# Transposes of an expert's activations placed between the products of a pair's sums

## The chip, the cores and the metric

The kernel runs on one core of one Trainium2 chip. The metric is the device time of one execution in microseconds (us); the median of several runs is compared. One more execution was taken with the hardware profiler on, and all rows below come from it.

## The reference

One layer of a streaming-encoder block over 512 tokens of width 1024: pooling and differential attention, cross-attention over 256 memory tokens, then a mixture of 32 experts of which each token takes four. The change lies in the experts alone:

```python
def expert_block(args):
    tok, g, e = args
    xb = xt[tok]
    hb = clamped_swiglu(xb @ w_gu[e] + b_gu[e])
    yb = hb @ w_down[e] + b_down[e]
    return yb * g[:, None].astype(yb.dtype)

y = jnp.zeros((T, D), h.dtype).at[row_tok].add(y_rows.reshape(n_rows, D).astype(h.dtype))
```

Here `T` is 512 and `D` is 1024; the tokens of an expert are gathered, go through gate-up, the clamped SwiGLU and down, are scaled by their gate and added back into `x`.

## The kernel before

The dense layers run first (`dense`, to about 410 us), then `experts` walks over the 32 experts, one stage for each, and a last stage without a gate-up. An expert has room for 96 tokens: a first part of 64 and a second part of 32, and the second part's products stand in a conditional block (`when`), entered only if the expert has more than 64 tokens. Weights come as 1 MB tiles in 17 shared buffers, eight `gu` tiles and four `dnw` tiles an expert, loaded by SyncE's queue as buffers come free.

Stage `e` runs gate-up of expert `e` and then down of expert `e - 1`. On TensorE its order is, as the code is written: the small products of `dispatch(e + 2)` that find slots and gates (tile `slots`), eight transposes of the gathered tokens (`to_features`: `xgT` in PSUM, then two VectorE multiplies at line 1010 write `xT`), six transposes of the activations of expert `e - 1` (`turn_act`: four into one PSUM tile `actT`, two into another, each copied to SBUF tile `aT` by one ScalarE instruction at line 1102), eight small products that put the biases into PSUM (`biases`), gate-up of the first part (`gate_up1`, weight tiles j = 0 to 7), gate-up of the second part (`gate_up2`), and `down`, which reads `aT`.

Experts go in pairs: `sums` gives each pair its tiles `ya`, `yb` and the one-hot `ohc`, which `down` fills through `split` (a ScalarE copy at line 120, then a VectorE subtraction at line 121, on the same PSUM bank). In an odd stage with `e > 2`, after j = 3, `combine_half` adds the pair before into `x`: for each of four token tiles `i` and two halves `h`, three products (`sum_up`'s parts) go into a PSUM tile `comb1`, and VectorE adds that to `x` (line 1162). There are 15 such stages (e = 3, 5, ..., 31) with 24 products and 8 additions each.

TensorE's order is the order in which the code is written: `queued` puts every matmul and transpose behind the one before. The other engines' instructions are put in order by the framework's scheduler, which works with times of its own; a few are pinned to their written place (`keep_in_program_order`, the scaling of the gathered tokens at line 999 among them).

PSUM tiles made by `bank` share four buffers (`ps1`), those made by `pair` share two. During gate-up one of the four holds the second part's accumulator (`pc`), so `comb1` turns over the other three; `actT`, `slots` and the two tiles of `down` come from the same four.

Of the kernel before, what the change touches and what calls it, by code (L numbers as in the profile page):

```python
# [24 lines left out]
KT = D // P  # L25
# [35 lines left out]
class Block:  # L61
# [904 lines left out]
    def slots(self, pt, n):  # L966

        nc = self.nc
        t = self.ms.tile([P, n, 2, 6], F32, name="slots")
        nc.vector.tensor_copy(t, pt)  # L970
        tok = self.ms.tile([P, n, 2], F32, name="tok", bufs=5)
        nc.vector.scalar_tensor_tensor(tok, t[:, :, :, 1], float(P), t[:, :, :, 0], op0=OP.mult, op1=OP.add)
        gat = self.ms.tile([P, n, 2], F32, name="gat", bufs=5)
        nc.vector.tensor_tensor(gat, t[:, :, :, 2], t[:, :, :, 3], op=OP.add)
        nc.vector.tensor_tensor(gat, gat, t[:, :, :, 4], op=OP.add)
        gi = self.ms.tile([CAP, n], I32, name="gi", bufs=5)
        nc.vector.tensor_copy(gi[0:64], tok[0:64, :, 0])
        nc.vector.tensor_copy(gi[64:96], tok[64:96, :, 1])

        nc.vector.scalar_tensor_tensor(tok, tok, -1.0, t[:, :, :, 5], op0=OP.add, op1=OP.add)  # L980
        return gi, gat, tok
# [114 lines left out]
    def turn_act(self, act, n):  # L1096
        nc = self.nc
        pt = self.bank("actT", (P, 4, P))
        for c in range(n):
            self.tr(pt[:, c], act[:, c * P:(c + 1) * P], self.ident)  # L1100
        aT = self.mw.tile([P, n, P], F32, name=f"aT{n}", bufs=1)
        nc.scalar.activation(aT, pt[:, :n], AF.Copy)  # L1102
        return aT

    def sums(self):

# [45 lines left out]
        nc = self.nc  # L1152
        self.add_sums(i, self.sum_up(i, self.pair("comb"), parts, True, True))

    def combine_half(self, i, h, parts):

        ps, n = self.bank("comb1"), len(parts)
        for k, (y, oh) in enumerate(parts):
            self.mm(ps, oh[:, i * P:(i + 1) * P], y[h] if isinstance(y, list) else y[:, h], start=k == 0,
                    stop=k == n - 1, skip_group_check=True)  # L1160
        xi = self.x_sb[:, i, 512 * h:512 * h + 512]
        self.nc.vector.tensor_tensor(xi, ps, xi, op=OP.add)  # L1162

# [12 lines left out]
    def experts(self):  # L1176
        nc = self.nc
        disp, xTs, xgs = {}, {}, {}

        def gather(e):  # L1180
            xgs[e] = self.gather(disp[e][0])

        def slots(e):
            return [t[:, 0] for t in disp[e][1:]]

        xTs[0] = self.first_features()
        acts, parts, xg = {}, {}, None
        for e in range(NE + 1):


            if e == 0:
                biases = self.load_down_biases()
            if e == 1:
                biases = self.down_biases(biases)
                for i in range(NT):
                    self.combine(i, [biases])
            if 0 < e < NE - 2:
                disp[e + 2] = self.dispatch(e + 2, 1)
            if 0 < e < NE:
                xTs[e] = self.to_features(xg)  # L1200
            if e:
                aT = [self.turn_act(t, n) for t, n in zip(acts.pop(e - 1), (4, 2))]

            if e < NE:
                gu = self.gu.pop(e)
                cond = lambda e=e: self.when(self.flag(e))
                if e + 1 < NE:
                    self.load_gate_up(e + 1)
                    if e:
                        gather(e + 1)  # L1210
                self.load_down(e)
                xT = xTs.pop(e)
                pa, pc = self.biases(self.pick[:, e:e + 1])
                for j in range(KT):
                    self.gate_up1(pa, xT, gu[j], j)
                    if e == 0 and j == 0:
                        self.count()
                    if e == 0 and j == 1:
                        disp[1] = self.dispatch(1, 1)
                        gather(1)  # L1220
                    if j == 3 and e % 2 and e > 2:
                        for i in range(NT):
                            for h in range(2):
                                self.combine_half(i, h, parts[e // 2 - 1])
                    if e == 0 and j in (1, 3, 5):
                        with cond():
                            for k in range(j - 1, j + 1):
                                self.gate_up2(pc, xT, gu[k], k)
                    if e == 0 and j == 2:
                        disp[2] = self.dispatch(2, 1)  # L1230
                    if j == 5 and e == 0:
                        disp[0] = self.dispatch(0, 1)
                        biases = self.round_down_biases(biases)
                    if j == 6 and e + 1 < NE:
                        xg = self.normed(xgs.pop(e + 1))
                act = self.swiglu(pa[:, 0], pa[:, 1], 512)
                with cond():
                    for k in range(0 if e else 6, KT):
                        self.gate_up2(pc, xT, gu[k], k)
                acts[e] = act, self.swiglu(pc[:, 0], pc[:, 1], 256)  # L1240

            if e:
                f = e - 1
                r = slice(64 * (f % 2), 64 * (f % 2) + 64)
                if f % 2 == 0:
                    parts[f // 2] = self.sums()
                p = parts[f // 2]
                self.down(*aT, self.dnw.pop(f), *slots(f), lambda f=f: self.when(self.flag(f)),
                          p[2 * (f % 2)], [t[r] for t in p[1]], last=e == NE)
        self.finish(parts[NE // 2 - 1])  # L1250
        self.overflow()
# [33 lines left out]
    def overflow(self):  # L1285
# [15 lines left out]
        n = nc.values_load(self.more[0:1, 0:1], min_val=0, max_val=NT * P * 4 // CAP)  # L1301
        with self.tc.For_i(0, n, 1):
# [14 lines left out]
            t = self.slot("own_t", [P, NT, NE])  # L1317
# [5 lines left out]
            with nc.allow_low_precision(reason="sums of one term that is not zero"):  # L1323
                for i in range(NT):
                    t = self.slot("own_v", [P, 6, NE])
# [4 lines left out]
            t = self.slot("own_p", [96, NE])  # L1330
# [4 lines left out]
            e = ms.tile([P, 1], F32, name="own_e", bufs=1)  # L1335
# [8 lines left out]
            w = []  # L1344
# [6 lines left out]
            gi, gat, tok = self.slots(pt, 1)  # L1351
# [4 lines left out]
                self.gate_up2(pc, xT, w[j], j)  # L1356
            act = self.swiglu(pa[:, 0], pa[:, 1], 512)
            act2 = self.swiglu(pc[:, 0], pc[:, 1], 256)
            aT, aT2 = self.turn_act(act, 4), self.turn_act(act2, 2)
            a, c, _ = self.sums()  # L1360
            c = [v[0:64] for v in c]
            self.down(aT, aT2, w[KT:], gat[:, 0], tok[:, 0], nullcontext, a, c)
            self.finish([a, c])

    def run(self):
# [41 lines left out]
```

## Time and profile before

| | us |
|---|---|
| median of 3 runs | 1485.63 |
| lowest, highest | 1483.84, 1486.21 |
| the profiled execution | 1483.18 |
| its span, first to last instruction | 1480.9 |

In that span TensorE (PE) is busy for 1428.7 us, VectorE (DVE) 700.9, ScalarE (ACT) 392.5, GpSimd (POOL) 31.8. The DMA engines move 455.61 MB, 307 GB/s of them from and to HBM over the span.

How to read the rows further down: PE is TensorE's matmuls, PEld its weight loads, which run beside the matmuls. Times in a timeline are in us from the start of the span, and successive instructions of one kind stand in one row, marked with x and their count. A matmul's duration holds its way through the array, so neighbours overlap; the distance from one start to the next is what the stream costs. Square brackets give the idle time of the engine ahead of the instruction and what ended it. Out<-in names the tile written and the tiles read; tile `gu` covers the weight tiles and both PSUM accumulators of gate-up, `comb` stands for `comb1`.

### The profile page before, as it was taken

How to read it: one execution, taken by the hardware profiler on the slowest of the kernel's cores; microseconds unless marked ns; L12 is line 12 of the kernel's file. 1: busy time of each engine (PE TensorE's matmuls, PEld its weight loads, DVE VectorE, ACT ScalarE, POOL GpSimd, SP SyncE). 2: the span in 40 equal slices, each digit the busy share in tenths (PEclk: the TensorE clock that was granted, in tenths of full speed). 3: DMA queues.
4: the chain of work that ended last, by engine and by line, in shares of the span. 5: the costliest groups of instructions: out<-in, count | busy, mean ns of one | idle time of the engine just before them, and what ended most of it. 6: DMA issues, size and time to landing. Idle time of an engine off the chain costs nothing. (4 is left out here: it accounts for less than half of the span.)

```text
span 1480.9 us, 22050 instructions
## 1 busy us (share of the span) xinstructions
PE 1428.7 (96%) x8940; PEld 744.3 (50%) x8940; DVE 700.9 (47%) x1700; ACT 392.5 (27%) x692; POOL 31.8 (2%) x49
## 2 busy tenths in 40 slices
PE   8999999999979999999999999999999999999994
PEld 7878788888333434344343443434343434434342
DVE  6857956452443534244353443433453434444334
ACT  6346635342112211111222121121212121121213
POOL 0000000000000000000000000000000000000000
PEclk9999999999989999999999999999999999999997
DMA  7222315066839898999999999999999999999941
GB/s 228 93 89 86 115 61 164 29 256 242 330 128 394 358 396 349 386 355 409 397 405 406 400 408 407 408 371 398 409 380 406 392 396 399 405 397 401 408 189 58
DMA packets 84310, 455.61 MB, mean 308 GB/s; under 512 B 14201, under 2 KB 14722, under 8 KB 35042
## 3 DMA queue, kind: packets, MB, share of 16 engines
q1 hardware_dynamic: 79330, 439.16, 75.0%
q0 software_dynamic: 3472, 12.29, 2.7%
q10 hardware_dynamic: 1392, 2.51, 0.5%
q8 instruction: 86, 1.41, 0.4%
q14 instruction: 30, 0.25, 0.0%
HBM read 449.71 MB, written 4.21 MB: 307 GB/s over the span
## 5 line engine op out<-in xcount | busy, mean ns | idle before, releaser
L107 PE MATMUL gu<-gu,xT 128*64 128x512 f32 (+1 forms) x3200 | 577.1, 594 | 3.2 <-DVE xT L1010 2.2
L107 PEld LDWEIGHTS gu<-gu,xT 128*64 128x64 f32 (+1 forms) x3200 | 177.5, 127 | 377.2 <-issue 349.8
L107 PE MATMUL down<-dnw,aT 128*32 128x256 f32 (+1 forms) x2288 | 300.0, 476 | 7.6 <-PEq L102 6.8
L1058 DVE TENSOR_SCALAR g<-gu 128x256 f32<-128x256 f32 x64 | 32.7, 552 | 392.7 <-PE gu L107 285.7
L107 PEld LDWEIGHTS down<-dnw,aT 128*32 128x32 f32 (+1 forms) x2288 | 120.7, 122 | 183.6 <-issue 145.4
L1060 ACT ACTIVATE s<-g 128x256 f32<-128x256 f32 x64 | 33.5, 523 | 386.0 <-DVE g L1058 385.9
L1162 DVE TENSOR_TENSOR x<-comb,x 128x512 f32<-128x512 f32 x120 | 82.0, 689 | 94.7 <-PE comb L107 94.6
L999 ACT ACTIVATE xg<-xg 96x1024 f32<-96x1024 f32 x31 | 35.7, 1150 | 246.3 <-DMA xg<-x_rows,gi 246.3
L120 ACT ACTIVATE yb<-down,gat 32x256 fp32r<-32x256 f32 x128 | 59.5, 465 | 124.6 <-DVE yb L121 86.0
L121 DVE SCALAR_TENSOR_TENSOR yb<-down,gat,yb 32x256 fp32r<-32x256 f32 x128 | 61.6, 482 | 55.0 <-ACT yb L120 53.5
L107 PE MATMUL comb<-ya,yb 128*128 128x512 f32 x256 | 83.5, 397 | 0.0
L118 DVE TENSOR_TENSOR w_lo<-w,w_hi 128x1024 fp32r<-128x1024 f32 x56 | 67.0, 1218 | 10.4 <-ACT w_hi L117 10.0
L120 ACT ACTIVATE ya<-down,gat 64x512 fp32r<-64x512 f32 x64 | 43.7, 683 | 65.6 <-PE down L107 64.8
L107 PEld LDWEIGHTS comb<-ya,yb 128*128 128x128 f32 x256 | 48.0, 188 | 22.7 <-issue 13.0
L117 ACT ACTIVATE w_hi<-w 128x1024 fp32r<-128x1024 f32 x56 | 56.7, 1052 | 4.2 <-DMA w<-in_w_ckv_dram 1.6
L121 DVE SCALAR_TENSOR_TENSOR ya<-down,gat,ya 64x512 fp32r<-64x512 f32 x64 | 48.0, 751 | 14.1 <-ACT ya L120 12.0
L107 PE MATMUL comb<-yb,ohc 128*128 128x512 f32 x128 | 49.9, 390 | 0.0
L1064 DVE TENSOR_TENSOR g<-gu,s 128x256 f32<-128x256 f32 x64 | 49.2, 844 | 1.5 <-ACT s L1060 1.5
L992 POOL DMA_INDIRECT xg<-x_rows,gi x31 | 28.5, 918 | 969.9 <-PE actT L111 508.0
L1102 ACT ACTIVATE aT<-actT 128x512 f32<-128x512 f32 x64 | 31.1, 489 | 43.7 <-PE actT L111 42.9
L111 PE MATMUL xgT<-ident,xg 96*128 96x96 f32 x256 | 36.0, 284 | 0.8 <-DVE xg L1031 0.8
L1010 DVE TENSOR_TENSOR xT<-xgT,g_ffn 128x384 f32<-128x384 f32 x64 | 34.7, 553 | 1.7 <-PE xgT L111 0.8
(340 smaller groups left out, 1676.8 us busy)
## 6 DMA issues: line engine op xcount, KB each, us to landing
gu<-in_w_gu_dram SPq DMA_DIRECT2D x256, 1024.0 KB, 17.4
dnw<-in_w_down_dram SPq DMA_DIRECT2D x128, 1024.0 KB, 19.9
w<-in_w_ckv_dram SPq DMA_DIRECT2D x8, 1024.0 KB, 5.2
w<-in_w_in_dram SPq DMA_DIRECT2D x7, 1024.0 KB, 5.8
w<-in_w_out_dram SPq DMA_DIRECT2D x4, 1024.0 KB
w<-in_w_cq_dram SPq DMA_DIRECT2D x4, 1024.0 KB, 6.2
w<-in_w_co_dram SPq DMA_DIRECT2D x4, 1024.0 KB
x<-in_x_dram SPq DMA_DIRECT2D x8, 256.0 KB, 6.0
```

What stands on the lines that cost most here:

```text
L107: self.pin(self.nc.tensor.matmul(*a, **k))
L111: self.pin(self.nc.tensor.transpose(*a))
L117: self.pin(nc.scalar.activation(hi, src, AF.Copy))
L118: self.pin(nc.vector.tensor_tensor(lo, src, hi.bitcast(F32), op=OP.subtract))
L120: nc.scalar.activation(hi, src, AF.Copy, scale=scale)
L121: nc.vector.scalar_tensor_tensor(lo, src, scale, hi.bitcast(F32), op0=OP.mult, op1=OP.subtract)
L999: self.nc.scalar.activation(xg[:, :D], xg[:, :D], AF.Copy, scale=xg[:, D:D + 1]))
L1010: nc.vector.tensor_tensor(xT[:, c], pt[:, c, :CAP], self.g3[:, c, None].to_broadcast([P, 4, CAP]), op=OP.mult)
L1058: nc.vector.tensor_scalar(g, gate, LIMIT, None, op0=OP.min)
L1060: nc.scalar.activation(s, g, AF.Sigmoid, scale=ALPHA)
L1064: nc.vector.tensor_tensor(g.rearrange("s (j b p) -> s j p b", p=P, b=2), r(up), r(s), op=OP.mult)
L1162: self.nc.vector.tensor_tensor(xi, ps, xi, op=OP.add)
```

## The change

`turn_act` becomes a generator that yields after each transpose, and `turn_acts` runs it for both activations and leaves the copied tiles in `self.aT`. In even stages, in stage 1 and in `overflow` it is run to its end at once, where the transposes stood before. In odd stages with `e > 2` nothing is transposed ahead of gate-up; `combine_half` instead takes one step of the generator after each of its products, from the second half of the first token tile on. With three products a half, the six transposes follow the three products of (i 0, h 1) and the three of (i 1, h 0); the copy of the first four comes with the fifth step, that of the last two with the seventh, after the first product of (i 1, h 1).

```diff
         for c in range(n):
             self.tr(pt[:, c], act[:, c * P:(c + 1) * P], self.ident)
+            yield
         aT = self.mw.tile([P, n, P], F32, name=f"aT{n}", bufs=1)
         nc.scalar.activation(aT, pt[:, :n], AF.Copy)
-        return aT
+        self.aT.append(aT)
+
+    def turn_acts(self, acts):
+
+        self.aT = []
+        for act, n in zip(acts, (4, 2)):
+            yield from self.turn_act(act, n)
...
-    def combine_half(self, i, h, parts):
+    def combine_half(self, i, h, parts, between):
...
                     stop=k == n - 1, skip_group_check=True)
+            if i or h:
+                next(between, None)
...
+            turned = None
             if e:
-                aT = [self.turn_act(t, n) for t, n in zip(acts.pop(e - 1), (4, 2))]
+                turned = self.turn_acts(acts.pop(e - 1))
+                if e == 1 or e % 2 == 0:
+                    for _ in turned:
+                        pass
...
-                                self.combine_half(i, h, parts[e // 2 - 1])
+                                self.combine_half(i, h, parts[e // 2 - 1], turned)
...
-                self.down(*aT, self.dnw.pop(f), *slots(f), lambda f=f: self.when(self.flag(f)),
+                self.down(*self.aT, self.dnw.pop(f), *slots(f), lambda f=f: self.when(self.flag(f)),
```

The rest of the diff gives `overflow`, which no token enters unless an expert has more than 96, the same generator run to its end.

## Rows read from the trace of the kernel before

**Rows 1.** The page: busy time (share of span, instructions); costliest groups.
```profile
PE 1428.7 (96%) x8940; PEld 744.3 (50%) x8940; DVE 700.9 (47%) x1700; ACT 392.5 (27%) x692; POOL 31.8 (2%) x49
...
L107 PEld LDWEIGHTS comb<-ya,yb 128*128 128x128 f32 x256 | 48.0, 188 | 22.7 <-issue 13.0
```

**Rows 2.** Waits, 425 to 1445 us: who waited for what, total us, times, longest.
```profile
PEld gu L107 <- DVE xT L1010: 15.5, 26, 0.7
...
PEld gu L107 <- DMA gu<-in_w_gu_dram: 3.9, 13, 0.4
...
PE gu L107 <- DVE xT L1010: 2.2, 12, 0.2
```

**Rows 3.** Timeline of PE, start of stage 5: start, us, instruction, idle before it.
```profile
546.65 1.10 PE L111 MATMUL xgT<-ident,xg 96*128 96x96 f32 x8
547.59 0.82 PE L111 MATMUL actT<-ident,g 128*128 128x128 f32 x6
548.34 0.95 PE L107 MATMUL gu<-bias,pick 96*32 96x512 bf16 x8
549.48 7.09 PE L107 MATMUL gu<-gu,xT 128*64 128x512 f32 x32 [0.19 <-DVE xT L1010]
```

**Rows 4.** Timeline of DVE, the same stretch.
```profile
547.37 0.28 DVE L961 TENSOR_SCALAR oh<-iota,slot_no 128x256 bf16<-128x256 bf16 x1
547.69 0.74 DVE L121 SCALAR_TENSOR_TENSOR ya<-down,gat,ya 64x512 fp32r<-64x512 f32 x1
548.46 0.16 DVE L975 TENSOR_TENSOR gat<-gat,slots 128x2 f32<-128x2 f32 x1
...
548.87 0.56 DVE L1010 TENSOR_TENSOR xT<-xgT,g_ffn 128x384 f32<-128x384 f32 x1
...
549.99 0.76 DVE L121 SCALAR_TENSOR_TENSOR ya<-down,gat,ya 64x512 fp32r<-64x512 f32 x1
```

**Rows 5.** Timeline of ACT, stage 5 to the end of its sums.
```profile
546.54 0.68 ACT L120 ACTIVATE ya<-down,gat 64x512 fp32r<-64x512 f32 x1 [0.31 <-PE down L107]
548.29 0.60 ACT L1102 ACTIVATE aT<-actT 128x512 f32<-128x512 f32 x1 [1.07 <-PE actT L111]
548.91 0.68 ACT L120 ACTIVATE ya<-down,gat 64x512 fp32r<-64x512 f32 x1
...
558.52 1.15 ACT L999 ACTIVATE xg<-xg 96x1024 f32<-96x1024 f32 x1 [8.52 <-DMA xg<-x_rows,gi]
```

**Rows 6.** Timeline of PE, the sums of stage 5 (first, last and what follows).
```profile
556.50 0.50 PE L107 MATMUL comb<-ya,yb 128*128 128x512 f32 x1
556.84 0.39 PE L107 MATMUL comb<-yb,ohc 128*128 128x512 f32 x1
...
557.53 0.40 PE L107 MATMUL comb<-yb,ohc 128*128 128x512 f32 x1
...
562.17 1.08 PE L107 MATMUL gu<-gu,xT 128*64 128x512 f32 x4
```

**Rows 7.** Timeline of DVE, the additions of stage 5.
```profile
557.50 4.78 DVE L1162 TENSOR_TENSOR x<-comb,x 128x512 f32<-128x512 f32 x7 [6.24 <-PE comb L107]
```

**Rows 8.** Timeline of PE in the dense part: transposes amid products of the sums' kind.
```profile
356.95 0.39 PE L107 MATMUL cops<-w_hi,col 128*128 128x512 f32 x1
357.18 0.60 PE L111 MATMUL h3T<-ident,x 128*128 128x128 f32 x4
357.53 0.47 PE L107 MATMUL cops<-w_hi,coh 128*128 128x512 f32 x1
357.85 0.39 PE L107 MATMUL cops<-w_lo,coh 128*128 128x512 f32 x1
```

**Rows 9.** Timeline of PE, start of gate-up in stage 31.
```profile
1405.02 0.95 PE L107 MATMUL gu<-bias,pick 96*32 96x512 bf16 x8
1405.80 7.04 PE L107 MATMUL gu<-gu,xT 128*64 128x512 f32 x32
```

**Rows 10.** Timeline of DVE, start of stage 31.
```profile
1404.91 1.02 DVE L1010 TENSOR_TENSOR xT<-xgT,g_ffn 128x384 f32<-128x384 f32 x2
```

More of the change, by code (lines that the diff above doesn't have):

```diff
@@ L1358, in overflow @@
             act2 = self.swiglu(pc[:, 0], pc[:, 1], 256)
-            aT, aT2 = self.turn_act(act, 4), self.turn_act(act2, 2)
+            for _ in self.turn_acts((act, act2)):
+                pass
             a, c, _ = self.sums()
             c = [v[0:64] for v in c]
-            self.down(aT, aT2, w[KT:], gat[:, 0], tok[:, 0], nullcontext, a, c)
+            self.down(*self.aT, w[KT:], gat[:, 0], tok[:, 0], nullcontext, a, c)
             self.finish([a, c])
```

## The prediction

> **What bounds the kernel now.** I read the page first: TensorE is busy for 1428.7 us of a span of 1480.9 [rows 1], so a change pays only where it shortens TensorE's own stream or a wait of it. The waits over the experts come next: of all the stretch the one that repeats is gate-up waiting for `xT`, 26 times on the weight load, at most 0.7 us, and part of it shows on the matmuls too; waits for weights are at most 0.4 us each [rows 2]. So in the experts TensorE sets the pace, DMA keeps ahead of it, and each stage has one small hole, at the start of gate-up. I then read the timelines of the three engines side by side around that hole and around the sums of stage 5, which stands for the odd stages.
>
> At the start of stage 5 the six transposes take TensorE from 547.59 to 548.34, 0.75 us. The bias products follow, and gate-up starts at 549.48, marked as waiting for `xT` [rows 3]. VectorE's first `xT` multiply runs from 548.87 for 0.56 us, to 549.43, and gate-up follows 0.05 us later: this multiply, not the transposes, lets gate-up start. What holds the multiply is VectorE's own queue: ahead of it stand the one-hots of a dispatch, the subtraction for `ya` (from 547.69 for 0.74 us) and small instructions for gates and indices from 548.46 on [rows 4]. Its input, the `xgT` transposes, is done before 547.8 (the eight start at 546.65 and last 1.10 us) [rows 3]. Nothing on that path reads `actT`.
>
> **What the change removes.** Six transposes, 0.75 us, leave the start of 15 odd stages. The bias products then start about 0.65 to 0.75 us earlier, but gate-up still waits for the `xT` multiply, whose predecessors on VectorE are fed by the down products' end (ScalarE's first `ya` copy at 546.54 [rows 5]), not by what was removed. So the hole grows by what was taken out, and in 14 stages I count a gain of 0.00 us. In stage 31, which has no dispatch left, `xT` is free earlier: the first multiply starts at 1404.91 [rows 10], and with 0.56 us for it and 0.05 to follow gate-up could start at 1405.52 against 1405.80 [rows 9]: a gain of 0.28 us, once.
>
> ScalarE loses the copy of `aT` at 548.29 that stands ahead of its second `ya` copy at 548.91 [rows 5]. That second copy shares a PSUM bank with VectorE's `ya` subtraction, which ends at 548.43 [rows 4], so it can move forward by some 0.45 us at most; who needs it is only the second `ya` subtraction, which is due after `xT`. Worth nothing by itself, and a risk (second rival).
>
> **What it adds.** The same six transposes now stand between products of the sums. First, their price on TensorE. The products run 0.23 us from start to start (three of them from 556.84 to 557.53 [rows 6]; the whole 24 from 556.50 to 562.17, 5.67 us). The trace has no lone transpose between two such products, but it has four in a row between products of the same shape and type in the dense part: from the product at 356.95 to the second product after them at 357.85 pass 0.90 us [rows 8], of which two product distances of 0.227 are not theirs, so 0.446 us for four, 0.11 each. The change of kind is in that: 0.23 from product to transpose, and after the transposes the first product is followed by the next only after 0.32 instead of 0.23 us. A lone transpose pays the change each time, so I bound it from 0.11 (the run's mean) to 0.14 (a run's mean plus one more 0.03 us change) and take 0.12: 6 x 0.12 = 0.71 us a stage.
>
> Can VectorE's additions hide that? Seven of them take 4.78 us, 0.683 each [rows 7], and three products take 0.68. The products are not held by the additions by more than 8 x 0.683 - 24 x 0.227 = 0.02 us a stage, so there is no slack to hide 0.71 us in. Nothing below zero is likely here either: a transpose can't make a product shorter.
>
> On weight loads a page speaks against the change. The rows show that the four transposes and the change of kind cost 0.446 us, no more than transposes do among themselves (0.75 us for six, 0.125 each, at the start of stage 5 [rows 3]). The Trainium skill, page "TensorE: Matmul & The Clock Gate", section "Measured speedup vs the span model", states that a weight load overlaps running matmuls only where its row group differs; ours all use 128 rows. By that rule a product's weight load (188 ns [rows 1]) would stick out behind each transpose of about 0.11 us by 0.08 us, 0.47 us a stage more; the rows on the four transposes speak against it, since they leave room for 0.03 at most. It is the third rival.
>
> Second, PSUM. Three of the four banks turn over in this stretch, and `actT` now takes two of the turns that were `comb1`'s. I lay the stage out from its start at 0, with the distances above, additions of 0.69 us that start 0.04 after the last product of a half ends, and a ScalarE copy of 0.60 us [rows 5]. Products of (0,0) start at 0, 0.34, 0.57; its addition runs 1.00 to 1.69 (as in rows 7: 557.50 is 1.00 after 556.50). Half (0,1) and its three transposes run 0.80 to 1.76; half (1,0) takes the first bank at 1.76, just free. The fourth transpose at 2.07 lets ScalarE copy from about 2.45 to 3.05. The fifth, due at 2.42, needs a bank: the one of (0,1) whose addition starts at 1.92 and ends at 2.61, so it waits about 0.25 us. Half (1,1), due at 3.06, takes the bank of the first `aT` copy at about 3.12: 0.07 more. After that banks are free in time. Together 0.32 us a stage. One end is nothing (0.00, if a bank is free in time after all); the other is that the scheduler gave the fifth transpose the bank that waits for the copy: until 3.10, 0.68 us. I take 0.32, since the additions come free first.
>
> Queues passed: the two `aT` copies now stand on ScalarE ahead of the pinned scaling of `xg` at line 999, which started at 558.52 [rows 5], 2.0 us into the sums. It will wait for them, up to about 561; its readers are the `xgT` transposes of the next stage, behind the other half of gate-up (7.09 us for four weight tiles [rows 3]) and `down`, so that costs nothing. If the scaling were first, the copies would wait for it till 559.67, 3.2 us into the sums, which keeps a bank 0.7 us longer; I let that widen the range. `down`, which reads `aT`, comes after the other half of gate-up, 7 us or more behind: covered. The additions come up to 1 us later; behind them on VectorE stand the one-hots of `down`, equally covered. SyncE's weight loads wait for TensorE's progress and follow it; the gather on POOL waits for `xgT`, which isn't moved.
>
> **The sum.** 0.71 + 0.32 = 1.03 us a stage. 14 x 1.03 + (1.03 - 0.28) = 15.2 us. On the profiled execution, 1483.18 becomes 1498.4; the median of the runs lies 2.45 above that execution, so 1500.8. With no bank wait: 14 x 0.71 + 0.43 = 10.4, to 1496.0; with the long one: 14 x 1.39 + 1.11 = 20.6, to 1506.2.
>
> **Rivals.** (1) Not slower: VectorE's order changes. If the scheduler, with times of its own, puts the first `xT` multiply ahead of the `ya` subtraction, as soon as `xgT` is there at 547.8, gate-up starts when the bias products end: 547.59 + 0.09 + 0.78 = 548.46, 1.02 us earlier (0.78 is what they take where nothing waits, from 1405.02 to 1405.80 [rows 9]; 0.09 is the change of kind that now stands between the six transposes and them). That pays for the sums' 1.03 us: about 1486, and without bank waits 14 x (0.71 - 1.02) = -4.3, 1481. It decides where `xT` comes over 0.8 us earlier. For it: the input is early. Against: what stands ahead of it on VectorE is not touched by the change, and its input was as early before. 14%: 9 within 0.2%, 5 faster.
> (2) Slower still: ScalarE's second `ya` copy, moved forward to about 548.45 and ready by 549.15, lets the scheduler place its subtraction (0.76 us [rows 4]) ahead of `xT`. Then gate-up is late by as much again: 14 x 0.76 = 10.6 more, 1511. Against: `xT` starts at 548.87, before that copy ends. 6%.
> (3) The exposed weight loads: 15 x 0.47 = 7 more, 1508. 3%.
>
> **How the numbers follow.** The forecast (1496 to 1506 by the bank wait's ends, a little more for lone transposes at 0.11 or 0.14 and for the scaling on ScalarE) holds 77%, and all of it is slower. About 0.2%, 3 us, is what a measurement of this kernel can tell from no change. Faster by more than that: 5%; within it: 9%; slower: 77 + 6 + 3 = 86%. The range 1492 to 1509 takes in the forecast with its bounds and the third rival, some 79%; the first and second are left out.
>
> **What would show it.** Right: in the changed kernel's odd stages gate-up still starts 0.05 us after the first `xT` multiply, the wait for `xT` is longer by about 0.7 us, the distance from the first product of the sums to the gate-up behind them is 6.4 to 7.1 us instead of 5.67, and a repeated wait stands at the fifth transpose. Wrong: gate-up starts earlier against the end of `down`; or the sums take 5.7 us with the transposes in; or gate-up starts later than now. An order of VectorE that differs ahead of `xT` would make all of the prediction's first half wrong.

## The result, and the profile after

| | before | after |
|---|---|---|
| median of 4 runs, us | 1485.57 | 1501.88 |
| lowest to highest | 1483.84 to 1486.21 | 1500.26 to 1506.54 |
| profiled execution (span) | 1483.18 (1480.9) | 1502.55 (1500.3) |

The ratio is 1.0122, with a 95% interval of 1.011 to 1.0134: 16.3 us slower, where 15.2 were forecast.

The waits of the changed kernel, 425 to 1460 us, stand against [rows 2] (who waited for what: total us, times, longest).

```profile
PEld gu L107 <- DVE xT L1010: 26.1, 28, 1.3
...
PE gu L107 <- DVE xT L1010: 11.8, 15, 0.8
...
PEld actT L111 <- DVE x L1171: 5.8, 15, 0.4
...
PEld gu L107 <- DMA gu<-in_w_gu_dram: 4.1, 14, 0.4
PEld comb L107 <- ACT aT L1103: 3.7, 15, 0.3
```

The wait for `xT` on the matmuls has gone from 2.2 to 11.8 us, 15 times, and two waits are new, each 15 times, once an odd stage: a transpose for an addition, a product of the sums for a copy of `aT`. Waits for weights are as short as they were.

The start of stage 5 after the change, TensorE first, to be laid beside [rows 3]:

```profile
548.45 1.11 PE L111 MATMUL xgT<-ident,xg 96*128 96x96 f32 x8
549.49 0.95 PE L107 MATMUL gu<-bias,pick 96*32 96x512 bf16 x8
551.28 7.09 PE L107 MATMUL gu<-gu,xT 128*64 128x512 f32 x32 [0.84 <-DVE xT L1010]
```

and VectorE in the same stretch, beside [rows 4]:

```profile
549.49 0.74 DVE L121 SCALAR_TENSOR_TENSOR ya<-down,gat,ya 64x512 fp32r<-64x512 f32 x1
...
550.67 0.56 DVE L1010 TENSOR_TENSOR xT<-xgT,g_ffn 128x384 f32<-128x384 f32 x1
...
551.33 0.76 DVE L121 SCALAR_TENSOR_TENSOR ya<-down,gat,ya 64x512 fp32r<-64x512 f32 x1
552.12 0.56 DVE L1010 TENSOR_TENSOR xT<-xgT,g_ffn 128x384 f32<-128x384 f32 x1
```

From the first `xgT` transpose to gate-up pass 2.83 us, as before (546.65 to 549.48). The six transposes are gone and the idle time ahead of gate-up has grown by the same 0.65 us, from 0.19 to 0.84. The first `xT` multiply stands behind the same `ya` subtraction as before. The second `ya` subtraction has moved forward, ahead of the second multiply, not of the first.

The sums of stage 5 on TensorE, beside [rows 6]:

```profile
558.30 0.50 PE L107 MATMUL comb<-ya,yb 128*128 128x512 f32 x1
...
559.34 0.27 PE L111 MATMUL actT<-ident,g 128*128 128x128 f32 x1
...
559.68 0.27 PE L111 MATMUL actT<-ident,g 128*128 128x128 f32 x1
...
560.39 0.27 PE L111 MATMUL actT<-ident,g 128*128 128x128 f32 x1
560.42 0.48 PE L107 MATMUL comb<-yb,ohc 128*128 128x512 f32 x1
560.98 0.33 PE L111 MATMUL actT<-ident,g 128*128 128x128 f32 x1
561.06 0.48 PE L107 MATMUL comb<-ya,yb 128*128 128x512 f32 x1
...
565.12 1.08 PE L107 MATMUL gu<-gu,xT 128*64 128x512 f32 x4
```

6.82 us instead of 5.67. A pair of product and transpose takes 0.34 us (559.34 to 559.68) where a product took 0.227. From 560.42 to the fifth transpose at 560.98 pass 0.56 instead of 0.32 us: it waits for its bank. What frees the banks is an addition, on VectorE's timeline beside [rows 7]:

```profile
560.23 0.69 DVE L1171 TENSOR_TENSOR x<-comb,x 128x512 f32<-128x512 f32 x1 [0.23 <-PE comb L107]
```

or a copy, on ScalarE's beside [rows 5]:

```profile
560.76 0.60 ACT L1103 ACTIVATE aT<-actT 128x512 f32<-128x512 f32 x1 [9.80 <-PE actT L111]
561.75 0.39 ACT L1103 ACTIVATE aT<-actT 128x256 f32<-128x256 f32 x1 [0.40 <-PE actT L111]
562.16 1.16 ACT L999 ACTIVATE xg<-xg 96x1024 f32<-96x1024 f32 x1
```

and a product's weight load (PEld) waits for the second of these copies:

```profile
562.19 0.19 PEld L107 LDWEIGHTS comb<-ya,yb 128*128 128x128 f32 x1 [0.25 <-ACT aT L1103]
```

The addition of half (0,1) ends at 560.92, the fifth transpose follows at 560.98. The second copy ends at 562.14, and half (2,0), which wants its bank, gets its weights at 562.19. The bank of the first copy, which ends at 561.36, goes to half (1,1); it starts at 561.41, 0.03 us behind the sixth transpose, as products there do, so this turn is hardly late. The scaling of `xg` comes behind both copies, as laid out.

Taken stage by stage from the two profiles, from one stage's `xgT` to the next's: even stages differ by at most 0.02 us, odd ones from 3 to 29 by 1.12 to 1.19, except stage 19 (2.86, see the end), stage 31 by 0.93. That makes 18.7 us of the span's 19.4 (17.0 without the excess of stage 19); the rest lies ahead of the experts, where nothing was changed.

### The profile page after: what moved, and what is told of

Same layout as the page of the kernel before. It is cut to its first block, busy times and chain, and to the rows that moved or that the text cites. A ratio compares the mean times of both kernels' runs of the same rounds, so it can differ in the third digit from the quotient of the medians.

```text
span 1500.3 us, 22051 instructions
## 1 busy us (share of the span) xinstructions
PE 1437.3 (96%) x8940; PEld 741.6 (49%) x8940; DVE 701.9 (47%) x1700; ACT 392.8 (26%) x692; POOL 31.8 (2%) x49
## 5 line engine op out<-in xcount | busy, mean ns | idle before, releaser
L107 PE MATMUL gu<-gu,xT 128*64 128x512 f32 (+1 forms) x3200 | 578.8, 595 | 12.6 <-DVE xT L1010 11.8
L107 PE MATMUL comb<-ya,yb 128*128 128x512 f32 x256 | 91.8, 426 | 0.0
L111 PE MATMUL actT<-ident,g 128*128 128x128 f32 x192 | 39.9, 281 | 1.2
```

The costliest lines, as they stand in the source:

```text
L107: self.pin(self.nc.tensor.matmul(*a, **k))
L111: self.pin(self.nc.tensor.transpose(*a))
```

## Experiments

The theory: what stands ahead of gate-up on TensorE in an odd stage is free, because `xT` comes later; the sums are held by TensorE, pay 0.12 us for each transpose, and beyond that wait for PSUM banks. Rivals: the transposes cost at the start what they take; single transposes among products cost more than in a run; the wait is not one for banks. Each ratio is to the kernel before, run again beside the experiment (medians 1483.70 to 1484.07 us), so kernels of different experiments are compared by ratios and by stages.

**e1_none: the transposes of odd stages left out.** On the kernel before:

```diff
-                aT = [self.turn_act(t, n) for t, n in zip(acts.pop(e - 1), (4, 2))]
+                turned = acts.pop(e - 1)
+                if e < 3 or e % 2 == 0:
+                    aT = [self.turn_act(t, n) for t, n in zip(turned, (4, 2))]
```

> The kernel before, with the six transposes (and their two copies) of the odd stages from 3 on left out; down then reads the activations of the expert before, so the output differs. Theory (the start of an odd stage is set by VectorE's queue up to the first multiply of xT, so what stands ahead of gate-up on TensorE is free): gate-up of stages 3 to 29 starts as long after the slots products as before (3.05 us in stage 5), only stage 31 gains 0.28 us; in all 1485.3, ratio 0.9998. Rival (the transposes cost their own time where they stood): 15 x 0.65 to 0.75 us less, about 1475, ratio 0.993.

Measured: 1485.41 us against 1483.79, ratio 1.0011 (1.0 to 1.0022): not faster. TensorE at the start of stage 5:

```profile
549.24 1.11 PE L111 MATMUL xgT<-ident,xg 96*128 96x96 f32 x8
550.27 0.95 PE L107 MATMUL gu<-bias,pick 96*32 96x512 bf16 x8
552.07 7.09 PE L107 MATMUL gu<-gu,xT 128*64 128x512 f32 x32 [0.85 <-DVE xT L1010]
```

2.83 us again from `xgT` to gate-up, with 90 transposes and 30 copies less in the program. The rival is out: at the start the transposes cost nothing, but for 0.28 us in stage 31. All that the change can do beyond that is add.

**e2_pair: `actT` in the pair of banks that lies idle.** On the changed kernel:

```diff
+        both = self.pair("actT", (P, 8, P)) if paired else None
...
+            yield from self.turn_act(act, n, both[:, 4 * c:4 * c + 4] if paired else None)
```

> The changed kernel, with the PSUM tiles of the six transposes of odd stages taken from the pair of banks that lies idle between the xT multiplies and the next stage, instead of the four shared banks; the transposes stand where the change put them. Theory (of the 1.15 us by which the sums grew, 0.71 are the transposes' own time and 0.43 are waits for a bank): sums of 6.4 us instead of 6.82, no wait at the fifth transpose, 15 x 0.43 = 6.5 us less than the changed kernel: 1495.4, ratio to the kernel before 1.0066. Rival (the 0.43 us are the price of single transposes between products, weight loads that stick out): sums stay at 6.8 us, 1501.9, ratio 1.011.

Measured: 1509.66 us, ratio 1.0168 (1.0151 to 1.0185): slower than either side expected, and sums longer by 1.43 to 1.47 us. TensorE in stage 5:

```profile
559.28 0.27 PE L111 MATMUL actT<-ident,g 128*128 128x128 f32 x1
559.31 0.48 PE L107 MATMUL comb<-yb,ohc 128*128 128x512 f32 x1
560.30 0.33 PE L111 MATMUL actT<-ident,g 128*128 128x128 f32 x1 [0.51 <-ACT aT L1104]
```

The fifth transpose now waits for the copy of the first four. Both lie in one tile, though in two banks, so the edit had put another wait in the place of the one it took away, and tells nothing on the rest. What it does show is the other end of my bounds: had the scheduler made the fifth transpose wait for the copy, the sums would be 0.3 us longer still. e8 below is the mended form.

**e3_block: all six in a run ahead of the sums.** On the changed kernel:

```diff
                     if j == 3 and e % 2 and e > 2:
+                        for _ in turned:
+                            pass
                         for i in range(NT):
```

> The changed kernel, with the six transposes in one run right ahead of the sums' first product instead of between the products. Theory: six in a run at 0.11 us each, 0.67 us a stage, and the banks are free in time (the copies to SBUF end 1.3 and 1.7 us after the run's start, the halves that need their banks come at 1.4 and 2.1): gate-up is held up for 6.35 us, 15 x 0.68 - 0.28 = 9.9 us over the kernel before, 1495.5, ratio 1.0067, the same as with the pair of banks. Rival (a transpose between two products costs more than one in a run, 0.08 us of exposed weight load each): this one is 7 us faster than the one with the pair of banks.

Measured: 1497.48 us, ratio 1.0104 (1.0078 to 1.013), the runs far apart (1493.71 to 1503.88, with mean granted clocks of 0.989 to 0.983 from the fastest to the slowest); the profiled one took 1493.71, span 1491.5. TensorE in stage 5:

```profile
557.27 0.87 PE L111 MATMUL actT<-ident,g 128*128 128x128 f32 x6
557.90 0.48 PE L107 MATMUL comb<-ya,yb 128*128 128x512 f32 x1
```

The odd stages are longer by 0.68 to 0.72 us, all but stages 9 and 31 (0.81, 0.50): about 0.63 for the run and 0.07 in the sums behind it (expected 0.68). So the 1.15 us are not the price of the transposes by themselves; in a run, with their banks free in time, they cost 0.70. What interleaving adds is parted by e8.

**e7_spread: one transpose after each of six halves.** On the changed kernel:

```diff
-            if i or h:
+            if (i or h) and k == n - 1:
                 next(between, None)
```

> The changed kernel, with one transpose after the last product of each half of a token tile (six halves, from the second on) instead of one after each product of two halves. TensorE's own work is the same, 0.71 us; the bank of the first four transposes is taken for four halves instead of 1.3, and by the layout of additions and copies each half still finds the bank of two halves before it just free (1.63 us against 1.60). Theory (waits for banks come where a bank is wanted sooner than an addition or a copy ends): waits of 0.1 to 0.2 us, sums of 6.5 us, 15 x 0.85 - 0.28 = 12.5 over the kernel before, 1498, ratio 1.0084. Rival (the longer a bank is away, the more is waited): sums of 7 us or more, 1505 or more.

Measured: 1506.43 us, ratio 1.0142 (1.0125 to 1.016), sums longer by 1.39 to 1.43 us: my layout missed, the rival held. Its waits:

```profile
PEld comb L107 <- DVE x L1171: 8.5, 30, 0.3
PEld actT L111 <- ACT aT L1103: 7.3, 15, 0.5
```

With `actT` away for four halves, two banks are left, and two products a stage wait for an addition, besides a transpose for the copy. I had set the bank 0.03 us late a half; the waits stand on the weight loads, 0.28 us each. The same 90 transposes cost more the longer they hold a bank.

**e8_pair_late: the idle pair, and both copies after the sixth transpose.** On the changed kernel:

```diff
+        if paired:
+            both = self.pair("actT", (P, 8, P))
+            for c in range(6):
+                act, b = acts[c // 4], c % 4
+                self.tr(both[:, c], act[:, b * P:(b + 1) * P], self.ident)
+                yield
+            for c, n in ((0, 4), (4, 2)):
+                aT = self.mw.tile([P, n, P], F32, name=f"aT{n}", bufs=1)
+                self.nc.scalar.activation(aT, both[:, c:c + n], AF.Copy)
```

> The changed kernel, with the six transposes of an odd stage written into the idle pair of banks as before, and both copies to SBUF only after the sixth transpose, so that no transpose waits for the copy of the four before it. Theory (0.71 us of the 1.15 are the transposes' own time, the rest waits for banks): no wait inside the sums, 6.4 us from their first product to gate-up instead of 6.82; 15 x 0.72 - 0.28 = 10.5 us over the kernel before, and some 2 us for one or two falls of the clock behind the longer holes at the stages' start: 1497 to 1499, ratio 1.0075 to 1.009. Rival (single transposes between products cost 1.15 us by themselves): sums of 6.8 us, 1502, ratio 1.011.

Measured: 1495.54 us, ratio 1.0077 (1.0056 to 1.0097). TensorE in the sums of stage 5:

```profile
560.10 0.50 PE L107 MATMUL comb<-ya,yb 128*128 128x512 f32 x1
...
562.16 0.27 PE L111 MATMUL actT<-ident,g 128*128 128x128 f32 x1
562.19 0.48 PE L107 MATMUL comb<-yb,ohc 128*128 128x512 f32 x1
562.50 0.27 PE L111 MATMUL actT<-ident,g 128*128 128x128 f32 x1
...
566.48 2.80 PE L107 MATMUL gu<-gu,xT 128*64 128x512 f32 x12
```

6.38 us, 0.71 more than before; over all odd stages 0.68 to 0.72. The transposes stand where the change put them, and the fifth (562.50) comes 0.34 us after the fourth like the others. So of the change's 1.15 us, 0.70 are the transposes themselves and 0.45 were waits for banks: laid beside each other start by start, the two kernels differ almost only behind the waits that e8 takes away. A lone transpose costs no more than one in a run (e3: 0.70).

**e4_early and e5_early_after: `xT` made early.** In the kernel before and in the changed one, `to_features` of the next expert stands ahead of `down`:

```diff
-            if 0 < e < NE:
-                xTs[e] = self.to_features(xg)
...
                 acts[e] = act, self.swiglu(pc[:, 0], pc[:, 1], 256)
+                if e + 1 < NE:
+                    xTs[e + 1] = self.to_features(xg)
```

> The kernel before (transposes of the activations ahead of gate-up in all stages), with to_features of the next expert moved ahead of down, so that xT is there long before gate-up needs it; the order of VectorE at a stage's start no longer holds TensorE. Theory (a hole of 0.36 us in odd and 0.23 us in even stages, waiting for xT, is all that TensorE idles at a stage's start): no wait for xT, 14 x 0.36 + 13 x 0.23 = 8 us less at most, less 0.1 us a stage for two more changes of kind: 4 to 8 us less, 1477.5 to 1481.5, ratio 0.995 to 0.997. Rival (something else is late next there, the weights or the banks): no gain, 1485.6.

> The changed kernel with the same move of to_features ahead of down. Theory (the removal of the six transposes at the start was worth nothing only because xT was late): with xT early the removal counts, 0.65 us a stage, the sums keep their 1.15 us, and no hole is left behind which the clock falls: 15 x 0.50 = 7.5 us over the kernel with that move alone, 1485 to 1489; 13 to 17 us less than the changed kernel. Rival (the loss came from the sums and would stay in full): 15 x 1.15 = 17 us over the kernel with that move alone.

Measured: e4 1481.21 us, ratio 0.9978 (0.9969 to 0.9988); e5 1489.05, ratio 1.003 (1.0019 to 1.004). Start of stage 5 of e4, then of e5:

```profile
547.88 0.35 PE L107 MATMUL slots<-tv,oh 128*128 128x6 bf16 x8
...
549.66 7.04 PE L107 MATMUL gu<-gu,xT 128*64 128x512 f32 x32
```

```profile
549.93 0.35 PE L107 MATMUL slots<-tv,oh 128*128 128x6 bf16 x8
...
551.00 1.46 PE L107 MATMUL gu<-gu,xT 128*64 128x512 f32 x6
```

Nothing waits for `xT` any more, and now the removal counts: 1.78 us from `slots` to gate-up with the transposes, 1.07 without. e5 lies 7.8 us above e4, 0.52 a stage (expected 7.5), against 16.3 for the same change without the move. That is the same finding from the other side: the same removal is worth 0 or 0.7 us, by whether `xT` is late. e4 has the lowest median of the study; its gain of 2.9 us falls short of the 4 to 8 expected. The eight `xgT` transposes take 1.06 us in their new place against 0.94, and the second part of gate-up ahead of them 7.00 against 6.89; the two changes of kind cost 0.2 us a stage, twice what I had set.

**e9_early_pair: e5 with the idle pair of e8.**

> Both together: the changed kernel, to_features ahead of down, the transposes in the idle pair of banks and their copies after the sixth. Theory: start 0.65 us shorter, sums 0.72 us longer, no waits: within 2 us of the kernel with the move alone, since a transpose costs TensorE the same wherever nothing waits; stages odd and even alike without holes. Rival (there is slack in the sums in which transposes are free): 15 x 0.65 = 10 us less than the move alone.

Measured: 1482.74 us, ratio 0.9988 (0.9978 to 0.9999), 1.5 above e4. With neither the hole nor the bank waits, it makes no odds, to within 0.1 us a stage, where the transposes stand: there is no slack in the sums.

**e10_filler and after_again: the hole filled.** On the changed kernel, twelve idle products in odd stages (the second is the changed kernel itself, once more):

```diff
                     for _ in turned:
                         pass
+                else:
+                    self.warm(12)
```

> The changed kernel, with twelve products of ones (128 columns, some 0.056 us each, 0.67 in all, into a PSUM tile that nobody reads) on TensorE where the six transposes stood at the start of odd stages. Theory (the hole there is free to fill, and the clock falls now and then because the hole has grown from 0.19 to 0.84 us): gate-up starts as long after the slots products as before, 3.04 us, sums of 6.82, no stage of 3.4 us at half clock behind a stage's start; as many us less as the changed kernel loses to such falls, 1.7 us each: 1500 to 1502 where the changed kernel has 1501.9. Rival (the falls have another cause than the hole): as many falls as in the other kernels with the longer hole (0, 1, 2, 4, 4 and 0 in their profiles). Second rival (the work in the hole costs): 15 x 0.67 = 10 us more, 1512.

> The changed kernel once more, beside the one with the filler, to see how often the clock falls behind the longer hole. Theory: sums and starts as in its first profile, some falls to half clock in stages behind the start, 1.7 us each; 1501 to 1504. Rival: no falls, 1500.2.

Measured: with the filler 1502.53 us (1502.27 to 1503.77), without it 1505.06 (1504.19 to 1508.62). Start of stage 5 with the filler:

```profile
550.36 0.35 PE L107 MATMUL slots<-tv,oh 128*128 128x6 bf16 x8
...
551.52 0.84 PE L107 MATMUL warm<-ones 128*128 128x128 bf16 x12
...
553.41 7.09 PE L107 MATMUL gu<-gu,xT 128*64 128x512 f32 x32 [0.17 <-issue]
```

0.76 us of useless products, and gate-up starts 3.05 us after `slots`, as before (546.43 to 549.48). The hole is free to fill: the 10 us of the second rival are not there. The four runs lie below the four of the changed kernel taken beside them, by 2.5 us in the median, and their mean granted clock is higher (0.988 to 0.99 against 0.984 to 0.987). That the filler makes the kernel faster is not shown by this, since the changed kernel's first four runs had a ratio of 1.0122, below the filler's 1.0130. Its time lies 0.5 us above what was expected; its profile spends 2.4 us more ahead of the experts than that of the kernel before.

## Why the prediction was right, and where it was off

**The start (0.00 us a stage): right.** 2.83 us from `xgT` to gate-up before, after, and with the transposes left out (e1). The bias products started 0.65 us earlier and the wait grew by 0.65; gate-up still starts 0.05 us behind the first `xT` multiply (551.23 to 551.28). Stage 31 gained 0.28 us, as worked out from [rows 9, 10]: from `xgT` to gate-up 2.50 us before and 2.22 after. The kernel before, then the changed kernel:

```profile
1403.30 1.13 PE L111 MATMUL xgT<-ident,xg 96*128 96x96 f32 x8
...
1405.80 7.04 PE L107 MATMUL gu<-gu,xT 128*64 128x512 f32 x32
```

```profile
1421.76 1.13 PE L111 MATMUL xgT<-ident,xg 96*128 96x96 f32 x8
...
1423.98 7.09 PE L107 MATMUL gu<-gu,xT 128*64 128x512 f32 x32 [0.21 <-DVE xT L1010]
```

**A transpose among products (0.12 us): right.** 0.34 less 0.227, and 0.70 for six in e8. The four in a row of [rows 8] gave the price, although no lone one stood in the trace. The third rival, weight loads that stick out by 0.08 us behind each, fell: 6 x 0.08 more isn't there, and e3 and e8 cost the same. On this the trace disagrees with what the Trainium skill, page "TensorE: Matmul & The Clock Gate", section "The mechanism" (the one ahead of the section that the prediction names), says in its list of what overlaps, that a weight load does so only where the row group differs: all of these use 128 rows, and in e8 a transpose with a product's load of 0.188 us behind it costs 0.117 us in all. The same section of the Trainium skill also lets a weight load that goes to the background weight buffer run ahead, which the prediction left out.

**The banks (0.32 us): right in kind, too small in size, and one wait in the wrong place.** 1.15 - 0.70 = 0.45 us. The wait of the fifth transpose was 0.24 us for the 0.25 laid out, ScalarE's copy ran from 2.46 to 3.06 us into the sums for 2.45 to 3.05. The 0.07 us laid out for half (1,1) came to 0.03. Missing were the slower start after a wait (0.085 us from the fifth transpose to its product instead of 0.027) and a wait that I had called free in time, that of half (2,0) for the second copy, which ends at 562.14: the product behind it comes 0.08 us late. With 0.45 the sum would be 14 x 1.15 + 0.87 = 17.0 instead of 15.2.

**The additions can't hide it: right.** In e8, where no bank is waited for, the sums still grew by 0.70 us, and e9 is not below e4.

**The rivals.** VectorE kept its order ahead of the first `xT` multiply, so the first and second did not come about. The second was near: the moved-up `ya` subtraction did pass the second `xT` multiply, where nobody waits. (The first rival's price without bank waits, -4.3, leaves out the 0.43 us of stage 31; nothing hangs on it.)

**Left out: the clock.** The sum had no term for it; in the profiled execution it took 1.7 us once. The four runs of 1500.26, 1501.22, 1502.55 and 1506.54 us had mean granted clocks of 0.99, 0.989, 0.988 and 0.985, so the longer runs are those with the lower clock.

**Luck.** The stages alone cost 17.0 us, 1.8 more than forecast, and the fall and what lies ahead of the experts made the two profiled executions differ by 19.4. That the medians lie only 16.3 apart, 1.1 from the forecast, goes with the scatter between executions (the profiled one of the kernel before was 2.4 us below its median), and not from the sum.

## What to carry to other kernels

Work taken off the bound engine just ahead of a wait is worth nothing until what it waits for is moved too: look at what ends the wait, and when. Work put between others costs its own time there if that engine is the bound one, and its buffers are then taken from those others: count the banks over the stretch before interleaving. The same edit can be worth 0 or 0.7 us by what surrounds it, so judge it stage by stage, from the trace.

## What was not expected of the hardware

In some stages the clock of TensorE fell just behind the longer hole. Granted clock and busy time in three stretches of the changed kernel's stage 19 (gate-up starts at 1018.94, after 0.84 us of waiting):

```profile
1018.00:1019.30 1.30, 0.46 (x4) 0.20 (x4) 1.22 (x6) 0.61 (x1) 0.89 (x1) 1.00 1.00 416
1019.40:1022.70 3.30, 3.30 (x10) 0.96 (x8) 1.29 (x4) 0.00 (x0) 0.00 (x0) 0.50 1.03 411
1022.80:1025.00 2.20, 2.20 (x14) 0.73 (x12) 0.00 (x0) 0.00 (x0) 0.00 (x0) 1.00 0.98 299
```

The last columns are the granted clock, the DMA share and GB/s: half clock (1.2 for 2.4 GHz) just behind the start of gate-up, and ten matmuls fall into 3.3 us where fourteen fall into 2.2 us at full clock. That stage took 1.7 us more than its fellows. Such falls, 0.05 to 0.38 us behind the start of gate-up, stand in the experts 1, 2, 2, 4, 0, 4 and 0 times in the profiles of the changed kernel (twice taken), e1, e2, e3, e7 and e8, all of which have the hole of 0.84 us in 14 stages; and not once in those of the kernel before, e4, e5, e9 and e10, whose holes are 0.2 us or none. Ten of these 13 stand in four stages, 13, 19, 25 and 27. By count, then, the falls go with the longer wait, 13 of 98 against 0 of 70, and where one came, the stage lost 1.7 us besides the wait. That the wait is their cause is not shown: e3 and e8 have it and no fall, e4, e5 and e9 were run on the chip of e8, and at 13 in 98 the 14 holes of e10's one profile would show no fall about one time in seven. Why the clock fell behind some of these waits and not behind the others is left open.
